# Four weight-stationary matmuls of a feature block: both 512-column ones ahead of both 256-column ones, where they alternated

## Chip, core and metric

The kernel runs on one core of one Trainium2 chip. The metric is the device time of one execution in microseconds.

## What is computed

The reference is one block of a hybrid model on 256 tokens of width 2048, in float32: a projection, a gated delta rule with eight heads, a sparse attention, an output projection with layer norm, and a gated feed-forward part with a second layer norm. Nearly all the work is in products of the activations with weights:

```
proj = x @ w_in[l]
...
merged = jax.nn.sigmoid(gate_a) * (o_a @ w_branch_a[l]) + jax.nn.sigmoid(gate_b) * (o_b @ w_branch_b[l])
x = layer_norm(DEEPNORM_ALPHA * x + merged @ w_out[l], ln1_g[l], ln1_b[l])
h_gate, h_up = jnp.split(x @ w_ffn_in[l], 2, axis=-1)
x = layer_norm(DEEPNORM_ALPHA * x + (jax.nn.silu(h_gate) * h_up) @ w_ffn_out[l], ln2_g[l], ln2_b[l])
```

## The kernel before

Each float32 operand is split in two float32r numbers, `hi` (rounded) and `lo` (the rest), and a product is made of three: hi x hi, hi x lo and lo x hi. Weights come from memory in chunks of 128 partitions by 1024 columns (512 KB): a load by SyncE into `raw`, a cast to `hi` on ScalarE (line 72), a subtraction to `lo` on VectorE (line 74). `raw`, `hi` and `lo` have four buffers each.

There are two ways to multiply. In `xs_mm` (lines 153 to 155) the activations lie still in TensorE and 512 weight columns move; every matmul has 512 columns. In `group_ws`, which the change touches, the weights lie still and the activations move. The activations' two halves lie next to each other in a tile `X2`, so that one matmul of 512 columns multiplies a `hi` weight tile with both halves (line 134), and one of 256 columns the `lo` weight tile with the high half alone (line 136); the latter adds to the first 256 columns of the same PSUM bank. A group has two output tiles of 128 features (`c` = 0, 1, one PSUM bank each) and sixteen steps `k` over the inner dimension, four chunks of four. Each `k` is a feature block of four matmuls, each with a weight tile of its own that is loaded ahead of it; two such neighbours, one of each width, are called a pair here. At the end of each chunk `tick()` lets generators ("chains") put in other work, on TensorE short float32 matmuls and transposes. `group_ws` is called in a first stage up to about 300 us (projection in feature-major order, mixed with the delta rule's chains) and in the feed-forward stage for 42 feature groups (42 x 32 = 1344 pairs), where the chains have no TensorE work.

An older helper, `ws_mm` (lines 117 to 120), has 256-column matmuls alone and runs at the start.

The order on TensorE and SyncE is that of the code (`manual_schedule`). On VectorE, ScalarE and GpSimd a scheduler lays the order from priorities and its own estimate of when each operation becomes ready; `chunk` raises the priority of its own operations by LEAD (70) places.

Of the kernel before, what the change touches and what calls it, by code (L numbers as in the profile page):

```python
# [17 lines left out]
P = 128  # L18
S = 256
D = 2048  # L20
KT = D // P
# [23 lines left out]
def block_kernel(ctx: ExitStack, tc: tile.TileContext, xT, x, cpack, onehot, relb, convw, alog, dtb, gnw,  # L45
                 ws, wws, win, wba, wbb, wo, wfi, wfg, wfo, ln1g, ln1b, ln2g, ln2b, out):
    nc = tc.nc
# [11 lines left out]
    def ps_acc():  # L59
        return acc.tile([P, 512], F32, name="acc", tag="acc")  # L60
# [4 lines left out]
    def chunk(src, pool=None, lead=LEAD):  # L65
        n = src.shape[1]
        pool = pool or wp
        with tc.high_priority(offset=lead):
            raw = wp.tile([P, n], F32, name="raw", tag="raw")
            nc.sync.dma_start(raw, src)  # L70
            hi = pool.tile([P, n], F32R, name="hi", tag="hi")
            nc.scalar.copy(hi, raw)  # L72
            lo = pool.tile([P, n], F32R, name="lo", tag="lo")
            nc.vector.tensor_sub(lo, raw, hi.bitcast(F32))  # L74
        return hi, lo
# [8 lines left out]
    def tick():  # L84
        clock[0] += 1
        for ch in list(chains):
            wait = ch[1]
            if isinstance(wait, str):
                if wait not in done or done[wait] >= clock[0]:
                    continue  # L90
            elif wait > clock[0]:
                continue
            try:
                n = next(ch[0])
            except StopIteration:
                chains.remove(ch)
                continue
            ch[1] = n if isinstance(n, str) else clock[0] + n
# [24 lines left out]
    def group_ws(srcs):  # L123

        pss = [ps_acc(), ps_acc()]
        for ci, src in enumerate(srcs):
            hi, lo = chunk(src)
            hv = hi.rearrange("p (k c) -> p k c", k=4)
            lv = lo.rearrange("p (k c) -> p k c", k=4)
            for kk in range(4):  # L130
                k = 4 * ci + kk
                for c in range(2):
                    cs = slice(c * P, (c + 1) * P)
                    nc.tensor.matmul(pss[c], hv[:, kk, cs], X2[k // 4][:, k % 4], start=(k == 0), stop=False,  # L134
                                     skip_group_check=True)
                    nc.tensor.matmul(pss[c][:, :S], lv[:, kk, cs], xh[:, k, :], start=False, stop=(k == KT - 1),  # L136
                                     skip_group_check=True)
            tick()
        return pss
# [59 lines left out]
    X2 = [xpool.tile([P, KT // 4, 2, S], F32R, name=f"X2_{i}") for i in range(4)]  # L199
# [11 lines left out]
    xh, xl = KV(XH), KV(XL)  # L211
# [46 lines left out]
    def groups(chain, ev, *args):  # L258

        for c in (0, 2):  # L260
            b = gidx[0]
            gidx[0] += 1
            start(chain(c, group_ws([wws[b, k] for k in range(4)]), ev if c else None, *args))
# [26 lines left out]
    pss = [ps_acc(), ps_acc()]  # L290
    srcs = w_in_block()
    for i in range(8):
        k0 = 2 * i
        parts = [srcs[i]] if i > 2 else [srcs[i][:, :512], srcs[i][:, 512:]]
        for j, src in enumerate(parts):
            k, n = k0 + j, 2 // len(parts)
# [567 lines left out]
    hv = sm.tile([P, 1], F32, name="hv")  # L864
# [98 lines left out]
    for f in range(2, FT):  # L963
        start(f_chain(f, group_ws([wfg[f - 2, k] for k in range(4)])))
# [115 lines left out]
```

## Time and profile before

| | |
|---|---|
| median of 3 runs | 1516.51 us (1516.35 to 1516.80) |
| the profiled execution | 1516.29 us |
| its span, first to last instruction | 1514.5 us |
| TensorE matmuls busy | 99% of the span |
| VectorE busy | 60% |
| ScalarE busy | 46% |

The time of an execution lies 1.8 us over the span of its trace. Matmuls overlap in the records (each shows its way through the array), so busy times of lines on TensorE add up to more than the time that passes; the distance between the starts of two neighbours is what one of them takes of the span. Starts in the rows have two decimals, so a single distance is known to 10 ns, and the mean of many better.

### The profile page before, as it was taken

The numbers are of one execution on the slowest core, as the hardware profiler recorded it, in microseconds if no ns is written. First come the engines' busy times: TensorE is split into PE (matmuls) and PEld (weight loads), VectorE is DVE, ScalarE is ACT, GpSimd is POOL, SyncE is SP. The second block draws the span as 40 slices with busy tenths as digits, with TensorE's granted clock in tenths as the row PEclk, the third lists the DMA queues.
The fourth block names the chain that finished last, engine by engine and source line by source line (L and its number), as shares of the span: only waits on it lengthen the run. The fifth ranks groups of instructions, "written<-read, shape, count | busy, mean of one in ns | idle before, by whom it ended". The sixth has DMA issues, their size and how long they took to land.

```text
span 1514.5 us, 20368 instructions
## 1 busy us (share of the span) xinstructions
PE 1499.0 (99%) x7920; PEld 1277.8 (84%) x7920; DVE 905.2 (60%) x1238; ACT 697.0 (46%) x914; POOL 40.2 (3%) x40
## 2 busy tenths in 40 slices
PE   9999999999999999999999999999999999999996
PEld 8888888888888888888888888888888888888885
DVE  6798984466464554575675555555555555445455
ACT  5765443445544444444444444444444444333341
POOL 0011010020100000000000000000000000000000
PEclk9999999999999999999999999999999999999999
DMA  8646574435465555558545555555555556656662
GB/s 287 196 154 201 175 189 153 154 126 165 156 209 193 195 183 194 193 184 295 200 157 190 183 184 192 182 188 187 184 191 183 189 186 243 193 192 194 194 206 98
DMA packets 86352, 284.59 MB, mean 188 GB/s; under 512 B 15776, under 2 KB 16840, under 8 KB 85488
## 3 DMA queue, kind: packets, MB, share of 16 engines
q1 hardware_dynamic: 77856, 273.39, 55.4%
q0 software_dynamic: 1360, 7.54, 1.6%
q10 hardware_dynamic: 7040, 2.36, 0.6%
q8 instruction: 62, 1.02, 0.3%
q14 instruction: 34, 0.28, 0.0%
HBM read 280.44 MB, written 2.82 MB: 187 GB/s over the span
## 4 chain that ended last, share of the span: by engine, by line
PE 97%; DMA 2%; DVE 0%; SPq 0%; issue 0%; ACT 0%; POOLq 0%; DVEq 0%; ACTq 0%
PE acc L134 31%; PE acc L136 15%; PE acc L153 15%; PE acc L155 15%; PE acc L154 15%; PE aux L587 1%; DMA raw<-in_win_dram 1%; DMA cp<-in_cpack_dram 0%; PE aux L802 0%; PE aux L741 0%; PE aux L481 0%; PE aux L456 0%; PE aux L568 0%; PE aux L501 0%; PE aux L653 0%; PE aux L467 0%
## 5 line engine op out<-in xcount | busy, mean ns | idle before, releaser
L74 DVE TENSOR_TENSOR lo<-raw,hi 128x1024 fp32r<-128x1024 f32 (+1 forms) x515 | 632.6, 1230 | 506.3 <-ACT hi L72 505.1
L72 ACT CAST hi<-raw 128x1024 fp32r<-128x1024 f32 (+1 forms) x515 | 538.8, 1047 | 650.2 <-PE acc L155 349.9
L134 PE MATMUL acc<-X,hi 128*128 128x512 f32 x1984 | 703.5, 399 | 0.0
L136 PE MATMUL acc<-X,lo 128*128 128x256 f32 x1984 | 556.4, 280 | 0.0
L134 PEld LDWEIGHTS acc<-X,hi 128*128 128x128 f32 x1984 | 372.7, 188 | 92.4 <-issue 1.0
L136 PEld LDWEIGHTS acc<-X,lo 128*128 128x128 f32 x1984 | 374.6, 189 | 0.0
L153 PE MATMUL acc<-hi,X 128*128 128x512 f32 x544 | 214.3, 394 | 0.0
L155 PE MATMUL acc<-hi,X 128*128 128x512 f32 x544 | 211.9, 389 | 0.0
L154 PE MATMUL acc<-lo,X 128*128 128x512 f32 x544 | 211.8, 389 | 0.0
L153 PE MATMUL acc<-hi,hH 128*128 128x512 f32 x352 | 137.0, 389 | 0.0
L155 PE MATMUL acc<-hi,hL 128*128 128x512 f32 x352 | 136.9, 389 | 0.0
L154 PE MATMUL acc<-lo,hH 128*128 128x512 f32 x352 | 136.9, 389 | 0.0
L155 PEld LDWEIGHTS acc<-hi,X 128*128 128x128 f32 x544 | 102.1, 188 | 21.5
L154 PEld LDWEIGHTS acc<-lo,X 128*128 128x128 f32 x544 | 102.2, 188 | 20.3
L153 PEld LDWEIGHTS acc<-hi,X 128*128 128x128 f32 x544 | 102.2, 188 | 20.3
L155 PEld LDWEIGHTS acc<-hi,hL 128*128 128x128 f32 x352 | 66.1, 188 | 13.9
L153 PEld LDWEIGHTS acc<-hi,hH 128*128 128x128 f32 x352 | 66.1, 188 | 13.7
L154 PEld LDWEIGHTS acc<-lo,hH 128*128 128x128 f32 x352 | 66.1, 188 | 13.7
L955 ACT COPY ft<-acc 128x256 f32<-128x256 f32 x84 | 31.0, 369 | 62.6 <-PE acc L136 62.6
L956 DVE TENSOR_TENSOR ft<-acc,ft 128x256 f32<-128x256 f32 x84 | 35.4, 422 | 26.7 <-ACT ft L955 26.7
L153 PE MATMUL acc<-hi,oh__104 128*128 128x512 f32 x128 | 50.4, 394 | 0.0
L155 PE MATMUL acc<-hi,ol__105 128*128 128x512 f32 x128 | 49.9, 390 | 0.0
(269 smaller groups left out, 864.8 us busy)
## 6 DMA issues: line engine op xcount, KB each, us to landing
raw<-in_wfg_dram SPq DMA_DIRECT2D x168, 512.0 KB, 4.0
raw<-in_win_dram SPq DMA_DIRECT2D x101, 512.0 KB, 3.4
raw<-in_wfo_dram SPq DMA_DIRECT2D x88, 512.0 KB, 4.4
raw<-in_wws_dram SPq DMA_DIRECT2D x80, 512.0 KB, 3.6
raw<-in_wo_dram SPq DMA_DIRECT2D x32, 512.0 KB, 4.4
raw<-in_wbb_dram SPq DMA_DIRECT2D x16, 512.0 KB, 4.3
raw<-in_wba_dram SPq DMA_DIRECT2D x16, 512.0 KB, 3.3
raw<-in_wfi_dram SPq DMA_DIRECT2D x8, 512.0 KB, 4.4
```

The lines of the kernel that those rows point to most:

```text
L72: nc.scalar.copy(hi, raw)
L74: nc.vector.tensor_sub(lo, raw, hi.bitcast(F32))
L134: nc.tensor.matmul(pss[c], hv[:, kk, cs], X2[k // 4][:, k % 4], start=(k == 0), stop=False, skip_group_check=True)
L136: nc.tensor.matmul(pss[c][:, :S], lv[:, kk, cs], xh[:, k, :], start=False, stop=(k == KT - 1), skip_group_check=True)
L153: nc.tensor.matmul(ps, xh, hv[:, kk], start=(k == 0), stop=False)
L154: nc.tensor.matmul(ps, xh, lv[:, kk], start=False, stop=False)
L155: nc.tensor.matmul(ps, xl, hv[:, kk], start=False, stop=(k == 2 * n - 1))
L587: nc.tensor.matmul(o, l, r, start=True, stop=True)
L955: nc.scalar.copy(t[:, i], ps[:, S:])
L956: nc.vector.tensor_add(t[:, i], ps[:, :S], t[:, i])
```

## The change

In each feature block the loop over `c` is made twice, first with the two 512-column matmuls, then with the two 256-column ones. The number, the shapes and the operands of all instructions stay; a line is added, so all later lines of the file have a number higher by one, and line 136 becomes line 137.

```diff
             for kk in range(4):
                 k = 4 * ci + kk
+                cs = [slice(c * P, (c + 1) * P) for c in range(2)]
                 for c in range(2):
-                    cs = slice(c * P, (c + 1) * P)
-                    nc.tensor.matmul(pss[c], hv[:, kk, cs], X2[k // 4][:, k % 4], start=(k == 0), stop=False,
+                    nc.tensor.matmul(pss[c], hv[:, kk, cs[c]], X2[k // 4][:, k % 4], start=(k == 0), stop=False,
                                      skip_group_check=True)
-                    nc.tensor.matmul(pss[c][:, :S], lv[:, kk, cs], xh[:, k, :], start=False, stop=(k == KT - 1),
+                for c in range(2):
+                    nc.tensor.matmul(pss[c][:, :S], lv[:, kk, cs[c]], xh[:, k, :], start=False, stop=(k == KT - 1),
                                      skip_group_check=True)
```

On TensorE, the first feature block of the first group and the start of the next one, before (`acc_528` and `acc_529` are the two PSUM banks, `hi_532` and `lo_534` the chunk):

```order
L120 MATMUL aux_125<-X2_3_88,ol__105 128x256
L134 MATMUL acc_528<-X2_0_85,hi_532 128x512
L136 MATMUL acc_528<-X2_0_85,lo_534 128x256
L134 MATMUL acc_529<-X2_0_85,hi_532 128x512
L136 MATMUL acc_529<-X2_0_85,lo_534 128x256
```

The same place in the changed kernel:

```order
L120 MATMUL aux_125<-X2_3_88,ol__105 128x256
L134 MATMUL acc_528<-X2_0_85,hi_532 128x512
L134 MATMUL acc_529<-X2_0_85,hi_532 128x512
L137 MATMUL acc_528<-X2_0_85,lo_534 128x256
L137 MATMUL acc_529<-X2_0_85,lo_534 128x256
```

The second 512-column matmul moved ahead of the first 256-column one; the wait for `lo_534` that the first matmul of line 136 carries moved with it. All blocks are alike.

On VectorE, in the first stage, about 77 to 84 us in the trace before, the operations between the 28th and the 29th subtraction to `lo` (`lo_1023` and `lo_1053`), and two more; `s_qT`, `s_e`, `s_mn` and `s_in` belong to chains. Before:

```order
L74 TENSOR_TENSOR lo_1023<-raw_1019,hi_1021 128x1024
L332 SCALAR_TENSOR_TENSOR s_qT_93<-pre_905,cw_109,s_qT_93 128x254
L332 SCALAR_TENSOR_TENSOR s_qT_93<-pre_905,cw_109,s_qT_93 128x253
L418 TENSOR_TENSOR s_e_101<-aux_931,gc_493 128x512
L418 TENSOR_TENSOR s_e_101<-aux_937,gc_493 128x512
L74 TENSOR_TENSOR lo_1053<-raw_1049,hi_1051 128x1024
L419 TENSOR_TENSOR s_mn_96<-cp_106,s_e_101 128x1024
L420 TENSOR_TENSOR s_in_99<-cp_106,s_e_101 128x1024
```

The same place in the changed kernel:

```order
L74 TENSOR_TENSOR lo_1023<-raw_1019,hi_1021 128x1024
L333 SCALAR_TENSOR_TENSOR s_qT_93<-pre_901,cw_109,s_qT_93 128x253
L333 SCALAR_TENSOR_TENSOR s_qT_93<-pre_905,cw_109,s_qT_93 128x255
L333 SCALAR_TENSOR_TENSOR s_qT_93<-pre_905,cw_109,s_qT_93 128x254
L419 TENSOR_TENSOR s_e_101<-aux_931,gc_493 128x512
L419 TENSOR_TENSOR s_e_101<-aux_937,gc_493 128x512
L333 SCALAR_TENSOR_TENSOR s_qT_93<-pre_905,cw_109,s_qT_93 128x253
L420 TENSOR_TENSOR s_mn_96<-cp_106,s_e_101 128x1024
L421 TENSOR_TENSOR s_in_99<-cp_106,s_e_101 128x1024
L74 TENSOR_TENSOR lo_1053<-raw_1049,hi_1051 128x1024
```

The two additions that make `s_mn` and `s_in` moved ahead of `lo_1053`; two operations on `s_qT` moved behind `lo_1023`.

## Rows read from the trace of the kernel before

**Rows 1.** The page: busy time of TensorE's matmuls and weight loads (PE, PEld) and of the other engines, and TensorE's granted clock in 40 slices, in tenths.

```profile
PE 1499.0 (99%) x7920; PEld 1277.8 (84%) x7920; DVE 905.2 (60%) x1238; ACT 697.0 (46%) x914; POOL 40.2 (3%) x40
...
PEclk9999999999999999999999999999999999999999
```

**Rows 2.** The chain of waits, its shares of the span by line.

```profile
by line: PE acc L134 30.8%; PE acc L136 15.5%; PE acc L153 15.4%; PE acc L155 15.3%; PE acc L154 15.3%; PE aux L587 1.2%; DMA raw<-in_win_dram 1.0%; DMA cp<-in_cpack_dram 0.5%; PE aux L802 0.5%; PE aux L741 0.4%; PE aux L481 0.3%; PE aux L4
```

**Rows 3.** The page's costliest groups: line, engine, operation, tiles, shape, count, busy us and mean ns of one, idle time before them.

```profile
L134 PE MATMUL acc<-X,hi 128*128 128x512 f32 x1984 | 703.5, 399 | 0.0
L136 PE MATMUL acc<-X,lo 128*128 128x256 f32 x1984 | 556.4, 280 | 0.0
L134 PEld LDWEIGHTS acc<-X,hi 128*128 128x128 f32 x1984 | 372.7, 188 | 92.4 <-issue 1.0
L136 PEld LDWEIGHTS acc<-X,lo 128*128 128x128 f32 x1984 | 374.6, 189 | 0.0
```

**Rows 4.** Everything that TensorE's matmuls waited for: us in total, times, longest.

```profile
PE aux L802 <- issue: 1.3, 2, 1.0
PE aux L288 <- DVE s_bm L285: 1.3, 1, 1.3
PE acc L120 <- DVE lo L74: 1.1, 4, 0.3
PE acc L117 <- ACT hi L72: 0.4, 1, 0.4
```

**Rows 5.** TensorE's matmuls in order of time in the feed-forward stage: start us, duration us.

```profile
900.20 0.28 PE L136 MATMUL acc<-X,lo 128*128 128x256 f32 x1
900.32 0.40 PE L134 MATMUL acc<-X,hi 128*128 128x512 f32 x1
900.56 0.28 PE L136 MATMUL acc<-X,lo 128*128 128x256 f32 x1
900.67 0.40 PE L134 MATMUL acc<-X,hi 128*128 128x512 f32 x1
900.91 0.28 PE L136 MATMUL acc<-X,lo 128*128 128x256 f32 x1
901.02 0.40 PE L134 MATMUL acc<-X,hi 128*128 128x512 f32 x1
901.26 0.28 PE L136 MATMUL acc<-X,lo 128*128 128x256 f32 x1
```

**Rows 6.** The groups of TensorE between 797.2 and 1263 us, the first 512-column row.

```profile
L134 PE MATMUL acc<-X,hi 128*128 128x512 f32 x1319 | 466.2, 399 | 0.0
```

**Rows 7.** A run of pairs in the first stage: two starts of line 134 with 28 others of that line between them.

```profile
157.20 0.39 PE L134 MATMUL acc<-X,hi 128*128 128x512 f32 x1
...
167.25 0.39 PE L134 MATMUL acc<-X,hi 128*128 128x512 f32 x1
```

**Rows 8.** Matmuls of one width: two 512-column ones with 29 others between them, and two 256-column ones with nine others between them.

```profile
20.63 0.28 PE L119 MATMUL aux<-X,oh__104 128*128 128x256 f32 x1
...
21.83 0.28 PE L120 MATMUL aux<-X,ol__105 128*128 128x256 f32 x1
...
499.18 0.39 PE L154 MATMUL acc<-lo,oh__104 128*128 128x512 f32 x1
...
505.98 0.39 PE L154 MATMUL acc<-lo,oh__104 128*128 128x512 f32 x1
```

**Rows 9.** Where the pairs of the feed-forward stage end and 512-column matmuls follow without a break; seven of these are left out before the last row.

```profile
1263.42 0.28 PE L136 MATMUL acc<-X,lo 128*128 128x256 f32 x1
1263.54 0.40 PE L153 MATMUL acc<-hi,hH 128*128 128x512 f32 x1
1263.78 0.40 PE L154 MATMUL acc<-lo,hH 128*128 128x512 f32 x1
1264.02 0.40 PE L155 MATMUL acc<-hi,hL 128*128 128x512 f32 x1
...
1265.87 0.39 PE L154 MATMUL acc<-lo,hH 128*128 128x512 f32 x1
```

**Rows 10.** Where 512-column matmuls end and pairs follow without a break.

```profile
788.47 0.39 PE L134 MATMUL acc<-X,hi 128*128 128x512 f32 x1
788.69 0.28 PE L136 MATMUL acc<-X,lo 128*128 128x256 f32 x1
788.81 0.40 PE L134 MATMUL acc<-X,hi 128*128 128x512 f32 x1
789.04 0.28 PE L136 MATMUL acc<-X,lo 128*128 128x256 f32 x1
```

**Rows 11.** A run's first pair behind float32 transposes in the first stage, and the start of the long run.

```profile
79.51 0.48 PE L134 MATMUL acc<-X,hi 128*128 128x512 f32 x1
79.82 0.28 PE L136 MATMUL acc<-X,lo 128*128 128x256 f32 x1
...
797.07 0.48 PE L134 MATMUL acc<-X,hi 128*128 128x512 f32 x1
```

**Rows 12.** VectorE and TensorE in the first stage: start us, duration us. The first `lo` row is `lo_1053`, whose chunk TensorE begins at 88.94 us; the last one belongs to the chunk that TensorE begins at 129.81 us.

```profile
80.70 1.22 DVE L74 TENSOR_TENSOR lo<-raw,hi 128x1024 fp32r<-128x1024 f32 x1
81.83 1.22 DVE L419 TENSOR_TENSOR s_mn<-cp,s_e 128x1024 f32<-128x1024 f32 x1
82.97 1.22 DVE L420 TENSOR_TENSOR s_in<-cp,s_e 128x1024 f32<-128x1024 f32 x1
...
88.94 0.40 PE L134 MATMUL acc<-X,hi 128*128 128x512 f32 x1
...
127.56 1.22 DVE L74 TENSOR_TENSOR lo<-raw,hi 128x1024 fp32r<-128x1024 f32 x1
...
129.81 0.39 PE L134 MATMUL acc<-X,hi 128*128 128x512 f32 x1
```

## The prediction

> **What bounds the kernel now.** I read the page first, for the busy shares [rows 1]: TensorE's matmuls are 99% of the span and the granted clock stands at 0.9 or more in every slice, so there is no stretch in which TensorE is slow for want of its clock. A busy share says little where matmuls overlap, so the chain of waits came next [rows 2]: it runs over TensorE lines almost alone, and the two lines of the change carry 30.8% and 15.5% of it. The list of what TensorE waited for [rows 4] is the third view, and the reader is to see how short it is: four entries, 4.1 us in all, none of them at line 134 or 136. In the stages of the change nothing but TensorE's own pace sets the end. So the question is only how far apart its matmuls start, and the fourth view is the order of starts in time, one row per matmul.
>
> **How far apart they start.** The start-to-start time is the price of a matmul here; the duration in a row overlaps with the next one and is no price. Four prices can be had from rows. Among themselves, 512-column matmuls with a new weight each start every 226.7 ns: 30 of them in 505.98 - 499.18 = 6.80 us [rows 8]. Among themselves, 256-column ones start every 120 ns: ten in 1.20 us [rows 8]. A pair of the two should then take 346.7 ns. It mostly doesn't: in the whole feed-forward stage 1320 pairs (1319 counted from 797.2 us on, and the first, at 797.07) take 1263.54 - 797.07 = 466.47 us, so 353.4 ns each [rows 6, 9, 11]. Within it the starts repeat after three pairs, 1.06 us [rows 5]: 120, 240, 110, 240, 110, 240 ns with the rows' rounding, on average 113 after a 256-column matmul and 240 after a 512-column one, so the one is followed some 7 ns too early and the other some 13 ns too late. But there is a second pattern of the very same instructions: 29 pairs from 157.20 to 167.25 us take 346.6 ns each [rows 7], exactly the sum of the two prices. Each of the 34 uninterrupted runs of pairs settles in one of the two and stays there; I went through all starts, and 21 runs with 1704 pairs show the slow pattern, 13 with 280 pairs the fast one. What puts a run into one or the other is how it was entered. So the extra 6.7 ns of a pair is no property of a matmul of 512 or 256 columns; it comes from the two widths following each other, and it can be absent.
>
> **The sum of what can move.** The chain has (30.8% + 15.5%) of 1514.5 us = 701.2 us on 1984 pairs [rows 2, 3]. At 346.67 ns they would take 687.8 us. Of the 13.4 us between, some belong to entering a run: behind a float32 piece the first start-to-start time is 310 ns, against 226.7, 0.08 us more [rows 11]; 32 of the 34 runs are entered that way, 2.6 us, and the change doesn't touch that. There remain 10.8 us, of which the feed-forward stage alone has 466.47 - 1320 x 0.34667 = 8.9 us. In blocks (two pairs) it is 10.8 / 992 = 10.9 ns over the 693.3 ns that four matmuls cost at their own prices.
>
> **The change part by part.** It adds and removes no instruction: 1984 matmuls of each width stay, with 1984 weight loads each [rows 3]. Per block of four it turns four changes of width (512 to 256, 256 to 512, twice) into two, and puts in one step from 512 to 512 and one from 256 to 256. The two new steps have rows among equals, 226.7 and 120 ns [rows 8]; that they cost the same inside a block of four is what I can't read off. Bounds: at the lower end all four steps cost their own price and 10.8 us go; at the upper end, the step to a second 512 directly behind a mixed run. There is one such place, at 1263.54 us, where the pairs end and 512-column matmuls begin [rows 9]: the first two take 240 ns each, and the first ten 2.33 us, 233 ns each, before they come down to 226.7. Against that stands the opposite switch at 788.47 us [rows 10]: out of a settled row of 512s the steps are 220, 120, 230 ns, no dearer than the prices. I take the middle: what is paid is paid per change of width, half the changes go, so half of 10.8 us. For the block that is 240 + 227 + 113 + 120 = 700 ns.
>
> What else moves: the wait for the low half of a chunk stands one matmul later, behind the second 512, which can only relax it. The order on VectorE and ScalarE is laid anew by the scheduler in the stage up to 240 us; SyncE's and GpSimd's stay. Going through both orders, no cast to `hi` gets more work in front of it, and the worst `lo` is the one shown under the change, with two additions of 1.22 us newly ahead, 2.4 us [rows 12]. TensorE reads that `lo` only at 88.94 us, and the operation it stands behind ended at 81.92 us, its own 1.2 us included: 7 us of cover. The thinnest cover in this stage is 1.0 us, a `lo` that ends at 127.56 + 1.22 = 128.78 us for a chunk that TensorE begins at 129.81 us [rows 12]; it gets no new work in front of it, and there the pairs already run in the fast pattern, so TensorE comes hardly sooner. I cost the new order at nothing; if that cover were gone, it would cost what the displaced additions last, 2.4 us once. A faster TensorE asks for chunks sooner by at most 1.5% (10.8 of 701 us); the queue has no row among TensorE's waits [rows 4].
>
> **Rivals.** (a) All of it goes: the block of four settles in a pattern without extra, as 13 runs did in their pairs. Then 1516.5 - 10.8 = 1505.7 us. For it: equal widths in a row settle at their price [rows 8]; against: they need some ten matmuls for it [rows 9], and here they have two. (b) Nothing changes: the extra belongs to the block, however it is ordered, or each matmul costs by its width alone. 1516.5 us. The Trainium skill, "TensorE: Matmul & The Clock Gate", section "Back-to-back issue gap", has such a rule: columns over 2.4 GHz and 2.5 ns more, whatever stands beside. By it a pair is 325 ns and its order is worth nothing; the trace disagrees, with 353.4 and 346.6 ns for the same instructions. For (b) remains that the slow pattern is the commoner one whatever a run came from. (c) Slower: a 512 directly behind a mixed stretch pays as at 1263.54 us, and the block never settles. With 240 ns for each 512, 113 for the 256 before a 512 and 120 for the other it takes 713 ns against 693.3 + 10.9 = 704 now, 992 x 9 ns = 8.9 us: 1525.4 us. It decides in the second 512: with the other three as here the block is dearer than now from 231 ns on, and by 3 us in all from 234 ns on; the mean of the ten is 233. Against it: after 512s the step to 256 and back is cheap [rows 10].
>
> **How the numbers follow.** The profiled execution took 1516.29 us, 1.8 us of it outside its span, and the median is 1516.51, so the sum holds for the median as it stands. Forecast: 1516.5 - 5.4 = 1511.1 us, chance 0.33. (a) 0.22, (b) 0.24, (c) 0.21. About 0.2%, 3 us, is what a measurement of this kernel can tell from no change. Faster by more than that are the forecast and (a), 0.55; (b) is 0.24; (c) 0.21. The low end lies just under (a), 1505.0; the high end takes in (b) and the milder part of (c), with the second 512 at 234 ns, 1520.0. Outside are some 0.04 below and 0.14 above.
>
> **What would show it.** In the changed kernel's starts, in the feed-forward stage: 512 to 512 at 227 ns, 256 to 256 at 120, and a block of about 700 ns for the forecast, 693 for (a), 707 for (b), 713 for (c); that stage then takes 660 times that. TensorE's list of waits should stay as it is; a new entry at line 134 or 137 released by VectorE before 240 us would mean that the new order on VectorE uncovered something. The prediction is wrong if the block has a price of its own that neither the equal rows nor the mixed ones show, or if different runs settle differently again, which would make the stage of 1320 pairs a matter of its entry alone.

## The result, and the profile after

The changed kernel takes 1508.32 us (median of 6 runs, 1507.61 to 1510.60) against 1516.09 (6 runs, 1515.55 to 1516.80); the ratio is 0.995, 95% interval 0.9939 to 0.9960. That is 7.8 us faster, where 5.4 were forecast. The profiled execution took 1507.61 us, its span 1505.8.

The page's busy times, as in [rows 1]:

```profile
PE 1491.0 (99%) x7920; PEld 1274.8 (85%) x7920; DVE 899.3 (60%) x1238; ACT 696.2 (46%) x914; POOL 40.3 (3%) x40
```

What TensorE's matmuls waited for, as in [rows 4] (us in total, times, longest):

```profile
PE aux L803 <- issue: 1.3, 2, 0.9
PE aux L289 <- DVE s_bm L286: 1.3, 1, 1.3
PE acc L120 <- DVE lo L74: 0.5, 1, 0.5
```

Nothing new waits: the new order on VectorE and ScalarE uncovered nothing. The time came from the distance between starts. TensorE's matmuls in order of time in the feed-forward stage; "x2" are two neighbours in one row, and the start is the first one's:

```profile
900.27 0.62 PE L134 MATMUL acc<-X,hi 128*128 128x512 f32 x2
900.74 0.40 PE L137 MATMUL acc<-X,lo 128*128 128x256 f32 x2
900.97 0.63 PE L134 MATMUL acc<-X,hi 128*128 128x512 f32 x2
901.44 0.39 PE L137 MATMUL acc<-X,lo 128*128 128x256 f32 x2
901.67 0.62 PE L134 MATMUL acc<-X,hi 128*128 128x512 f32 x2
```

Two blocks take 1.40 us here. Over the whole stage, from its first start to the first matmul of the next one:

```profile
795.00 0.70 PE L134 MATMUL acc<-X,hi 128*128 128x512 f32 x2
...
1254.88 0.40 PE L154 MATMUL acc<-hi,hH 128*128 128x512 f32 x1
```

That is 459.88 us for 660 blocks, against 466.47 [rows 9, 11]: 6.59 us of the 8.7 by which the spans differ. Past its entry a block takes 696.7 ns, 3.3 ns over the sum of the four prices, and not 13.3 as in the slow pattern [rows 5]. All 34 runs settle in this one pattern; there is no second one any more. By the starts, the first stage gave 1.2 us: there a block gains 10 ns where the slow pattern stood and loses 3.3 where the fast one did. Another 0.8 us is the moment at which the first run starts, 36.09 us against 36.92, and has nothing to do with the change: up to there the instructions of all engines and their order are the same in both kernels, and over all profiled executions of this study the moment lies between 36.09 and 38.85 us. Without it 7.9 us remain, near the 7.8 of the medians. So stages are compared below by their own length.

### The profile page after: what moved, and what is told of

It is laid out like the page before. It is cut to its first block, busy times and chain, and to the rows that moved or that the text cites. A ratio compares the mean times of both kernels' runs of the same rounds, so it can differ in the third digit from the quotient of the medians.

```text
span 1505.8 us, 20462 instructions
## 1 busy us (share of the span) xinstructions
PE 1491.0 (99%) x7920; PEld 1274.8 (85%) x7920; DVE 899.3 (60%) x1238; ACT 696.2 (46%) x914; POOL 40.3 (3%) x40
## 4 chain that ended last, share of the span: by engine, by line
PE 97%; DMA 1%; DVE 1%; ACT 0%; issue 0%; SPq 0%; POOLq 0%; DVEq 0%; ACTq 0%
PE acc L134 31%; PE acc L156 15%; PE acc L154 15%; PE acc L155 15%; PE acc L137 15%; PE aux L588 1%; DMA raw<-in_win_dram 1%; PE aux L803 0%; PE aux L742 0%; DMA s_vT<-in_xT_dram 0%; PE aux L482 0%; PE aux L457 0%; PE aux L569 0%; PE aux L502 0%; DVE lo L74 0%; PE acc L120 0%
## 5 line engine op out<-in xcount | busy, mean ns | idle before, releaser
L134 PE MATMUL acc<-X,hi 128*128 128x512 f32 x1984 | 625.9, 397 | 0.0
L137 PE MATMUL acc<-X,lo 128*128 128x256 f32 x1984 | 390.0, 278 | 0.0
L134 PEld LDWEIGHTS acc<-X,hi 128*128 128x128 f32 x1984 | 302.1, 189 | 2.1 <-ACT hi L72 0.7
L155 PE MATMUL acc<-lo,oh__104 128*128 128x512 f32 x128 | 49.8, 389 | 0.0
L959 ACT ACTIVATE ft<-ft 128x256 f32<-128x256 f32 x42 | 17.6, 418 | 45.4 <-DVE ft L957 45.4
```

Of the source, the lines that this page charges most:

```text
L134: nc.tensor.matmul(pss[c], hv[:, kk, cs[c]], X2[k // 4][:, k % 4], start=(k == 0), stop=False, skip_group_check=True)
L137: nc.tensor.matmul(pss[c][:, :S], lv[:, kk, cs[c]], xh[:, k, :], start=False, stop=(k == KT - 1), skip_group_check=True)
L155: nc.tensor.matmul(ps, xh, lv[:, kk], start=False, stop=False)
L959: nc.scalar.activation(t[:, 0], t[:, 0], AF.Silu)
```

## Experiments

All but the two with 384 columns keep the operands and alter only the order in `group_ws`, by two helpers that issue one matmul each. The cuts of code below are shortened and written with these helpers on both sides:

```python
def wide(kk, c):      # 512 columns, line 134
def narrow(kk, c):    # 256 columns, line 136
```

In the table w is a 512-column matmul and n a 256-column one; "stage" is the feed-forward stage as above, and "extra" is what four matmuls take over 693.3 ns, the sum of their prices among equals, in the settled part of it. A block in the order w w n n is called a 2-2 block.

| kernel | order | stage, us | block, ns | extra, ns | time, us (runs) |
|---|---|---|---|---|---|
| before | w n w n | 466.47 | 706.7 | 13.3 | see above |
| changed | 2 w, 2 n | 459.88 | 696.7 | 3.3 | 1508.32 (6) |
| four_wide | 4 w, 4 n | 463.17 | 701.7 | 8.3 | 1511.59 (5) |
| eight_wide | 8 w, 8 n | 460.97 | 698.3 | 5.0 | 1509.60 (5) |
| sixteen_wide | 16 w, 16 n | 459.34 | 695.8 | 2.5 | 1507.52 (4) |
| turned_banks | 2 w, 2 n, banks turned | 459.88 | 696.7 | 3.3 | 1508.71 (1) |
| crossed_banks | w n w n, banks crossed | 466.47 | 706.7 | 13.3 | 1518.22 (1) |
| entry_block | w n w n, one 2-2 block a group | 461.86 | 706.7 and 693.3 | 13.3 and 0 | 1511.36 (6) |
| one_flip | w n w n, one 2-2 block in all | 457.73 | 693.3 | 0 | 1507.60 (4) |
| flip_and_blocks | first stage 2 w, 2 n; then as one_flip | 457.73 | 693.3 | 0 | 1506.59 (5) |

**Do fewer changes of width cost less?** The theory of the prediction was that the extra is paid per change of width.

```diff
-                for c in range(2): wide(kk, c); narrow(kk, c)      # in each kk
+            for k0 in range(0, 4, 2):                               # four_wide; eight_wide: step 4
+                for f in (wide, narrow):
+                    for kk in range(k0, k0 + 2):
+                        for c in range(2): f(kk, c)
```

> Four 512-column matmuls (two feature blocks), then their four 256-column ones, half as many changes of width as in the changed kernel. Theory 1, the extra is paid per change of width: the changed kernel's block takes 696.7 ns, 3.3 over the sum of its own prices (693.3), with two changes; here two changes stand in two blocks, so 695.0 ns a block, about 1.7 us under the changed kernel, 1506.6 us. Theory 2, the extra is paid while a row of equal width settles, up to ten matmuls at 233 ns as in rows 9: each 512 pays about 6 ns, the block takes some 705 ns and the time comes back to about 1516 us.

> All eight 512-column matmuls of a chunk, then its eight 256-column ones; the changes of width are a quarter of the changed kernel's. Theory 1 (per change of width): 3.3 ns on four blocks, 694.2 ns a block, 2.5 us under the changed kernel, about 1505.8 us. Theory 2 (settling): eight 512s at 233 ns and eight 256s at 120 give 706 ns a block, about 1517 us. If a chunk's lo half were needed later than now it would only help; no new wait is expected.

four_wide came out at 0.9969 (0.9957 to 0.9981) of before and eight_wide at 0.9958 (0.9944 to 0.9972), both above the changed kernel's 0.995. The intervals touch; the stages, 463.17 and 460.97 us against 459.88, decide it. So the theory per change of width falls: half the changes cost not 1.7 but 8.3 ns a block. Theory 2, that a row of equal width pays until it settles, holds in part. Starts in eight_wide, eight neighbours to a row:

```profile
901.10 1.11 PE L137 MATMUL acc<-X,lo 128*128 128x256 f32 x8
902.05 2.00 PE L132 MATMUL acc<-X,hi 128*128 128x512 f32 x8
903.89 1.12 PE L137 MATMUL acc<-X,lo 128*128 128x256 f32 x8
904.84 2.00 PE L132 MATMUL acc<-X,hi 128*128 128x512 f32 x8
```

The eight 256s take 0.95 us (8 x 120 ns are 0.96); the eight 512s take 1.84, where 8 x 226.7 ns are 1.81. Start by start the row of 512s runs 233, 236, 228, 233, 231 and then 226 and 227 ns: it pays 27 ns over its first five steps and then nothing. The first two 256s behind it take 113 and 119 ns and give 7 to 8 of them back, so 20 ns a row are left. Ten steps, as [rows 9] show, were not needed, and one price of 20 ns for a row of any length would make longer rows the cheaper ones.

**Longer rows.** Every second chunk issues its 256s first, so that 16 of a width are neighbours.

```diff
-                for f in (wide, narrow):                           # eight_wide
+                for f in ((narrow, wide) if ci % 2 else (wide, narrow)):
```

> As the kernel with eight and eight, but every second chunk has its 256-column matmuls first, so that 16 of a width follow each other. There the eight 512s behind eight 256s paid 20 ns in their first five steps and nothing after. Theory 2 as it now stands (a settling row of 512s pays 20 ns once per row, however long): 20 ns on 32 matmuls, 2.5 ns a block, 695.8 ns, 1507.5 us. If the row of 256s, twice as long, or the turn of the order disturbs as well, 698 ns as with eight, about 1509.6 us. The first chunk's low half is used as late as with eight; in every second chunk it is used first, which could show as a wait for VectorE.

The block takes 695.8 ns as expected, the time is 0.9941 (0.9925 to 0.9958) of before, and no wait was added at lines of the groups. Once a row is long enough to settle it pays 20 ns once, net. That doesn't say why two and two cost less than four and four.

**Is it the PSUM bank?** The change also altered which matmuls follow each other in one bank. Two kernels part banks from widths.

```diff
+            wide(kk, 0); wide(kk, 1); narrow(kk, 1); narrow(kk, 0)      # turned_banks
+            wide(kk, 0); narrow(kk, 1); wide(kk, 1); narrow(kk, 0)      # crossed_banks, not in a group's first block
```

> As the changed kernel, but the two 256-column matmuls in turned order: 512 to bank 0, 512 to bank 1, 256 to bank 1, 256 to bank 0. Widths follow each other as in the changed kernel, but both changes of width now stay in one PSUM bank, where in the changed kernel every step goes to the other bank. Theory 1 (widths): 696.7 ns a block as in the changed kernel, 1508 us. Theory 3, the extra is paid where a matmul adds to the bank that the one ahead of it still writes: 706.7 ns a block, as in the slow pattern of before, about 1518 us.

> Widths alternate as before, but in each feature block except a group's first: 512 to bank 0, 256 to bank 1, 512 to bank 1, 256 to bank 0, so that a 256 no longer follows the 512 of its own bank (the step from one block to the next now stays in bank 0). Theory 1 (widths): the slow pattern remains in the long run, 353.4 ns a pair, 1516 us, or a run is entered otherwise and takes 346.7. Theory 3 (banks): three of four places where a bank follows itself are gone or moved, one a block is left of two; the pair drops to 350 ns or less in every run, about 1511 us.

turned_banks:

```profile
900.01 0.63 PE L132 MATMUL acc<-X,hi 128*128 128x512 f32 x2
900.48 0.40 PE L137 MATMUL acc<-X,lo 128*128 128x256 f32 x2
900.71 0.63 PE L132 MATMUL acc<-X,hi 128*128 128x512 f32 x2
901.18 0.39 PE L137 MATMUL acc<-X,lo 128*128 128x256 f32 x2
901.41 0.40 PE L132 MATMUL acc<-X,hi 128*128 128x512 f32 x1
```

crossed_banks:

```profile
900.12 0.40 PE L132 MATMUL acc<-X,hi 128*128 128x512 f32 x1
900.36 0.28 PE L137 MATMUL acc<-X,lo 128*128 128x256 f32 x1
900.47 0.40 PE L132 MATMUL acc<-X,hi 128*128 128x512 f32 x1
...
901.18 0.40 PE L132 MATMUL acc<-X,hi 128*128 128x512 f32 x1
```

The first is the changed kernel's pattern, two blocks in 1.40 us, the second is the slow one, three pairs in 1.06 us; the stages take 459.88 and 466.47 us, the very lengths of the two kernels with the same widths. The banks make no difference here. (Its 1518.22 us, in a single run, go back to a first run that starts at 38.85 us, 1.9 us later than before.)

**Does the entry decide between the slow and the fast pattern?** In before both patterns have the same instructions. One block per group in the changed order enters each run anew:

```diff
             for kk in range(4):
+                if ci == 0 and kk == 0:
+                    wide(kk, 0); wide(kk, 1); narrow(kk, 0); narrow(kk, 1)
+                else:
                     for c in range(2): wide(kk, c); narrow(kk, c)
```

> The widths alternate as before, except in the first feature block of each group, which has the changed kernel's order; so a run is entered anew every 16 blocks, in the feed-forward stage 42 times. Theory 4, how a run is entered decides between the two patterns of before and the run keeps it: the runs fall in the fast pattern at least in part, where before the whole feed-forward stage had the slow one; if all do, a pair takes 346.7 ns there, 8.8 us less, about 1507 us. Rival: alternation comes to the slow pattern by itself whatever went ahead, and the short fast runs of before are the exception; then the pairs behind the first block take 353.4 ns and the time is 1515.5 to 1516.5 us.

It came to 0.9968 (0.9956 to 0.9979) of before, half of what was to be had, and the trace shows why: in the feed-forward stage each such block turns the pattern, from slow to fast and from fast to slow, and the pairs keep it until the next one. The first two of the 41 turning blocks of that run, with the pairs around them:

```profile
798.96 0.40 PE L132 MATMUL acc<-X,hi 128*128 128x512 f32 x1
799.20 0.28 PE L137 MATMUL acc<-X,lo 128*128 128x256 f32 x1
799.32 0.40 PE L132 MATMUL acc<-X,hi 128*128 128x512 f32 x1
799.56 0.28 PE L137 MATMUL acc<-X,lo 128*128 128x256 f32 x1
799.67 0.63 PE L132 MATMUL acc<-X,hi 128*128 128x512 f32 x2
800.14 0.39 PE L137 MATMUL acc<-X,lo 128*128 128x256 f32 x2
800.37 0.40 PE L132 MATMUL acc<-X,hi 128*128 128x512 f32 x1
...
810.08 0.40 PE L132 MATMUL acc<-X,hi 128*128 128x512 f32 x1
...
810.77 0.63 PE L132 MATMUL acc<-X,hi 128*128 128x512 f32 x2
811.23 0.40 PE L137 MATMUL acc<-X,lo 128*128 128x256 f32 x2
811.47 0.40 PE L132 MATMUL acc<-X,hi 128*128 128x512 f32 x1
...
812.53 0.40 PE L132 MATMUL acc<-X,hi 128*128 128x512 f32 x1
```

Ahead of 799.67 two pairs take 0.71 us, the slow pattern. From 800.37 to 810.77 stand 30 pairs in 10.40 us, 346.7 ns each, the fast one. Behind the second block three pairs take 1.06 us again.

But a 2-2 block does not turn every run. Of 15 such blocks in the first stage of this trace that have settled pairs on both sides, 12 turned the pattern and three did not. At 49.69 us the slow pattern stays, three pairs in 1.06 us ahead of the block and behind it; at 61.38 us the fast pattern stays, three pairs in 1.04 us ahead and two in 0.69 behind, and so it does at 161.43 us:

```profile
48.63 0.40 PE L132 MATMUL acc<-X,hi 128*128 128x512 f32 x1
...
49.69 0.62 PE L132 MATMUL acc<-X,hi 128*128 128x512 f32 x2
...
50.39 0.40 PE L132 MATMUL acc<-X,hi 128*128 128x512 f32 x1
...
51.45 0.40 PE L132 MATMUL acc<-X,hi 128*128 128x512 f32 x1
...
60.34 0.39 PE L132 MATMUL acc<-X,hi 128*128 128x512 f32 x1
...
61.38 0.63 PE L132 MATMUL acc<-X,hi 128*128 128x512 f32 x2
...
62.09 0.40 PE L132 MATMUL acc<-X,hi 128*128 128x512 f32 x1
...
62.78 0.40 PE L132 MATMUL acc<-X,hi 128*128 128x512 f32 x1
```

The place in the cycle seems to decide. The steps of the slow pattern repeat as 233, 117, 241, 120, 236, 113 ns. Wherever the slow pattern turned it had just made the steps 236, 113 or 233, 117; where it did not turn it had just made 241, 120. Where the fast pattern did not turn, its pairs were equal, 230 and 117 ns; where it turned, pairs of 350 and 344 ns alternated. In the feed-forward stage of this kernel and of the next two the slow pattern always meets its block behind 236, 113, so these turns are no test of the place, and three exceptions are few: it is not shown.

**One block.** If a run keeps its pattern, a single block that turns it is enough. one_flip has it in the second feed-forward group and nowhere else, in four matmuls out of 7920:

```diff
-    def group_ws(srcs):
+    def group_ws(srcs, flip=False):
...
+                if flip and ci == 0 and kk == 0:
...
-        start(f_chain(f, group_ws([wfg[f - 2, k] for k in range(4)])))
+        start(f_chain(f, group_ws([wfg[f - 2, k] for k in range(4)], f == 3)))
```

> The order of before everywhere, except in one feature block: the first one of the second feed-forward group, 4 matmuls of 7920. In the kernel with one such block a group each of them turned the pattern, slow to fast and fast to slow. Theory 4 (a run keeps its pattern, and such a block turns it): from there on some 1300 pairs take 346.7 instead of 353.4 ns, 8.7 us less, about 1507.7 us. Rival (the slow pattern comes back by itself after some time): the stage stays near 466 us and the time near 1516 us.

It took 1507.60 us, 0.9941 (0.9927 to 0.9954) of before. TensorE's starts at the beginning of the stage, at the turning block, 200 us behind it, and at the end of the stage:

```profile
796.81 0.48 PE L132 MATMUL acc<-X,hi 128*128 128x512 f32 x1
...
799.71 0.63 PE L132 MATMUL acc<-X,hi 128*128 128x512 f32 x2
...
1000.09 0.40 PE L132 MATMUL acc<-X,hi 128*128 128x512 f32 x1
...
1000.43 0.39 PE L132 MATMUL acc<-X,hi 128*128 128x512 f32 x1
...
1000.78 0.40 PE L132 MATMUL acc<-X,hi 128*128 128x512 f32 x1
...
1254.54 0.40 PE L165 MATMUL acc<-hi,hH 128*128 128x512 f32 x1
```

457.73 us, 8.74 less than before and 2.15 less than with the change in every block. At 1000 us two pairs take 0.69 us, where the slow pattern takes 0.71, and the length of the stage leaves no room for a return: 1320 pairs of 346.7 ns are 457.6 us.

**Both.** The changed order where runs are short and each is entered anew, the single turning block where one run is long:

> The changed kernel's order in the first stage, where every run took 3.3 ns a block over the sum of the prices, and the order of before with one turning block in the feed-forward stage. If theory 4 holds: 1.3 us less than with the turning block alone (2.4 us of extra in the first stage become 1.1), 2.2 us less than the changed kernel (660 x 3.3 ns), about 1506.3 us. If the entry into the feed-forward stage depends on the order in the first stage, the block turns it the wrong way and the time is about 1515 us.

1506.59 us, 0.9935 (0.9921 to 0.9948) of before, the fastest kernel of this study; on the same chip as one_flip it is 1.0 us ahead of it, and its first stage is 1.2 us shorter.

**Does the short matmul have to be as short as the load of the next weights?** Two kernels with 384 columns in place of 256.

```diff
-                nc.tensor.matmul(pss[c][:, :S], lv[:, kk, cs], xh[:, k, :], ...
+                nc.tensor.matmul(pss[c][:, :384], lv[:, kk, cs], X2[k // 4][:, k % 4].rearrange("p a b -> p (a b)")[:, :384], ...
```

> The alternation of before with 384 columns in place of 256 (it multiplies the low half of the weights with 128 columns of the activations' low half as well, which the reference's product leaves at rounding size). By width alone such a matmul has 384/512 of 213.3 ns and the 13.3 ns that rows 8 show on top, 173.3 ns, and a pair 400.0 ns. Theory 5, the extra of mixed widths comes up where the short matmul is no longer than the load of the next weights beside it (a 256 is followed after 113 to 120 ns, a 384 after 173): a pair takes 400.0 ns in every run. Theory 1 (any change of width pays): 403 to 407 ns. The whole comes to 1516 + 1984 x 0.05 = 1610 us or 5 to 13 us more.

> Eight 512-column matmuls, then eight of 384 columns, to have the price of 384 among equals, which the sum for the alternation with 384 took at 173.3 ns. If it is 173.3, the alternation's 413.3 ns a pair holds 13.3 ns of extra and mixed widths pay without the short one being as short as a weight load; if it is some 180 to 187 ns, 384 has a price of its own and the pair had little or no extra.

(Both also multiply the low weights with part of the low activations, as the first of the two texts says.) The sum in the first of the two texts is off: 1984 x 0.05 us are 99 us. From the two patterns of before, 353.4 and 346.7 ns, to 400 ns it is 94 us, so its total of 1610 stands. The kernel took 1636.13 us, because most pairs take 413.3 ns: 1320 of them from 837.70 to 1383.37 us, which is 413.4 with the entry. There are two patterns here too: 31 of the 34 runs show 413.3 ns, three with 152 pairs 406.7. The long run:

```profile
837.70 0.48 PE L132 MATMUL acc<-X,hi 128*128 128x512 f32 x1
...
1383.37 0.40 PE L159 MATMUL acc<-hi,hH 128*128 128x512 f32 x1
```

One of the three, with 55 pairs between the two starts, 22.37 us:

```profile
134.88 0.39 PE L132 MATMUL acc<-X,hi 128*128 128x512 f32 x1
...
157.25 0.40 PE L132 MATMUL acc<-X,hi 128*128 128x512 f32 x1
```

eight_384 took 1626.73 us:

```profile
900.34 2.01 PE L132 MATMUL acc<-X,hi 128*128 128x512 f32 x8
902.19 1.58 PE L137 MATMUL acc<-X,lo 128*128 128x384 f32 x8
903.60 2.01 PE L132 MATMUL acc<-X,hi 128*128 128x512 f32 x8
```

The 384s of the stage's first row take 173 to 175 ns each, so 173.3 ns among equals is borne out, and by it the alternation holds 13.3 ns of extra a pair in its common pattern, twice that of the slow pattern with 256, and 6.7 in the other. In the settled stage, as in the rows above, the eight 384s take 173 to 185 ns, 177 on average, and the eight 512s 231 on average instead of 226.7: a block takes 816.7 ns, 16.7 over the sum, where eight_wide pays 5.0. So the forecast of no extra fails. Whether the load of the next weights plays a part stays open, because the record of such a load is 188 ns long [rows 3]: a matmul of 173 ns is still the shorter of the two, and the theory's condition was not reversed.

## Why the prediction was right, and where it was off

**What bounds the kernel:** right. TensorE's distance between starts set the end; the chain, the waits and the other engines are as before.

**The two patterns:** right, and the most useful thing read from the trace of before. That the extra is no property of the instructions and that a run keeps the pattern in which it was entered was argued from 34 runs; one_flip shows it, with four matmuls that move 8.7 us. The split of the slow pattern into 240 and 113 ns was a matter of the rows' rounding: in the unrounded trace the steps are 233, 117, 241, 120, 236 and 113, on average 236.7 after a 512 and 116.7 after a 256. The sum of a pair is the same, and so is the 700 ns of the block.

**The sum of what can move:** right where it was tested. 10.8 us stood there; one_flip's stage gave back 8.74 of the 8.9 us put down to it.

**New order on VectorE and ScalarE at nothing:** right, no wait was added to those of [rows 4]. The thinnest cover, that of the chunk begun at 129.81 us before, went from 1.26 to 0.93 us as counted to the first 256-column matmul.

**Half of the extra goes:** this is the term that was mis-sized. The block was put at 700 ns and takes 696.7; 3.3 ns of extra are left, not 6.7, and over the 660 blocks of the feed-forward stage that is 2.2 of the 2.4 us by which the time was missed. The block stands midway between the forecast's and the 693.3 of rival (a). It has a price of its own that neither the equal rows nor the mixed ones show, which the prediction itself named as a sign that it is wrong. The step behind it, that the extra is paid per change of width, is wrong and came near by luck: four and four have half as many changes and pay 8.3 ns a block. The single steps were wrong as well: instead of 240, 227, 113, 120 ns two successive blocks run 233, 236, 116, 113 and 232, 231, 113, 119 by the starts. A row of two 512s doesn't get the price of 512s among equals; the sum comes out low because the 256s are followed early.

**Rival (c), slower:** its mechanism exists. A 512 behind a row of 256s does pay, in eight_wide 20 ns a row, net; in four_wide, whose rows end before they settle, it is 17. Both are slower than the changed kernel by it. At a length of two 3.3 ns a block are left, less than the alternation had.

**What stays open:** why widths in this order settle in this pattern. Banks were excluded by runs, a part of the weight loads was not. What in TensorE keeps a rhythm over 1300 pairs, why a 2-2 block turns it and whether the place in the cycle decides, no run here shows.

## What to carry to other kernels

Where TensorE bounds a kernel, read the distance between starts and not the busy time, and compare mixed sequences with the sum of what each matmul takes among equals; a few ns per matmul over thousands of them are a change that no list of waits shows. Look whether the same instructions run at two paces in one trace: then the pace is a state that can be entered, and one moved instruction may be worth as much as a new order everywhere. Whether it is must be read from the trace each time: the same block left three runs in their pattern. A pattern that settles by itself, as two and two did, is the safer choice where runs are short and often interrupted; in one long run the turning block gained more, but it depends on how that run is entered and, as it seems, on the place of the block.

## What the runs showed of the hardware that was not expected

- The same alternation of 512 and 256 columns holds either of two steady rhythms, 353.3 or 346.7 ns a pair at a granted clock of 1.0, and one block in another order can switch it back and forth: 41 times of 41 in the feed-forward stage of entry_block, 12 of 15 in its first stage.
- The extra over the sum of single prices doesn't fall with the number of changes of width: 13.3 or 0, 3.3, 8.3, 5.0 and 2.5 ns a block for rows of 1, 2, 4, 8 and 16.
- 384 columns alternating with 512 cost 13.3 ns a pair over the sum in 31 runs and 6.7 in three; 256 columns cost 6.7 or nothing.
- The settled cycles are whole multiples of 6.67 ns: 120, 226.7, 346.7, three slow pairs 1060, two 2-2 blocks 1393.3, the pairs with 384 columns 413.3 and 406.7.
